# A feed-forward by seven block products instead of eight, and a mixing product cut in two

## The chip, the cores and the metric

One Trainium2 chip, of which the kernel uses one core. The metric is the device time of one execution in microseconds; the time before is the median of three runs. An engine's name stands for its instruction queue: PE (matrix products), DVE and POOL (elementwise), ACT (functions and copies), SP (issues the DMAs).

## What is computed

Two blocks follow each other on 1024 tokens of width 1024, all in float32. Only the parts that the change touches are quoted in full:

```python
def hybrid_layer(x, c, ...):                       # block 1
    ...
    y_att = dsa_attention(...)                     # 8 heads of 64
    y_rwkv = rwkv7_group(...)                      # 8 heads of 64
    mix = jnp.concatenate([y_att, y_rwkv], axis=-1) @ w_out
    x = x + g_m * rms_norm(mix, mix_post_norm)
    hf = rms_norm(x, ffn_pre_norm) * (1 + sc_f) + sh_f
    f = (jax.nn.silu(hf @ w_ffn_gate) * (hf @ w_ffn_up)) @ w_ffn_down   # D_FF = 2816
    return x + g_f * rms_norm(f, ffn_post_norm)
```

Block 2 (`second_block`) normalises that x, multiplies it by `w_in` (a gated convolution, a latent attention and two gates), mixes, adds, and has a feed-forward of its own of the same sizes, with a causal convolution of width 3 in its middle. A gated embedding product ends it.

## The kernel before

**Products.** Every float32 factor is held as two parts, a high one rounded by ACT and a low one, the rest, by a subtraction on POOL or DVE. A product is three MATMULs (high by high, high by low, low by high) summed in PSUM: `mm3`, lines 101 to 103. A MATMUL has 128 rows to contract, 128 columns on the left and 512 on the right.

**Seven for eight.** Where both factors are cut into 2 x 2 blocks, seven products of sums of blocks replace eight. Block 2's feed-forward does so already. `up7` multiplies a weight's block sums by those of the activations, which an `Ops` object holds: per pair of token tiles seven sums of quarters (A11, A12, A22, S1 to S4), each in two parts. `Ops.put` writes rows that come with features on partitions, and `Ops.put_pair` transposes two tiles of tokens, forms the sums and splits them; of its elementwise steps four a pair are POOL's (lines 257, 270, 273). `down7` does the second product: per group of features it loads rows of the weight and of the features, forms the operands with `sub` and `op` (lines 401, 407, 409), multiplies (lines 284 to 286, `mm7`) and adds into accumulators (437, 439). The features lie in DRAM (`f_d`) between the two.

**Mixing.** Attention and RWKV run beside each other; their outputs go to DRAM (`y_att_d`, `y_rwkv_d`). `prologue` brings in the RWKV half (k = 4 to 7 of eight chunks of 128) and its weights while the last attention blocks run, through two raw buffers and four `yl` buffers. Behind attention come the four attention chunks, each multiplied by its softmax reciprocals (`yr`, a broadcast load), and the weights k = 0 to 3. Then per tile of 128 tokens `row_product` sums all eight chunks, 48 MATMULs; `post_add` takes squares (ACT), a root (POOL, lines 110 and 111), scales (DVE, 543) and adds x (POOL, 544); the tile is stored to `x1d`; `renorm` (554, 556) prepares the feed-forward's input, and `put_T` transposes it into `h`, a `Tok`, which holds tokens as they are.

**FFN1.** `ffn1` (lines 514 to 532) goes over 22 chunks of features in groups of two or three: gate and up products by `fm`, SiLU and product, then `down`, which adds to eight accumulators. In the last group `done1` adds x, stores to `x2d`, and `renorm` and `put_T` prepare block 2's input. Block 2's first stage, `local`, reads that and weights of `w_in_2`.

**Order.** No table sets it. The program's order is what the scheduler starts from; it moves an instruction ahead where its operands and buffers allow, and each engine then runs its queue in order. What a tile pool shares memory with, and how many buffers a name has, therefore decides where loads stand on SP. `c.wlayout(a, b)` opens a pool of a raw and b split weight buffers, `c.layout` shares the eight PSUM banks out.

Of the kernel before, what the change touches and what calls it, by code (L numbers as in the profile page):

```python
# [8 lines left out]
FP = mybir.dt.float32  # L9
FR = mybir.dt.float32r  # L10
# [14 lines left out]
class Core:  # L25
# [337 lines left out]

def halves(x):

    x = x.rearrange("p (g e t) -> p g e t", e=2, t=128)
    return x[:, :, 0], x[:, :, 1]


def down7(c, ap, rings, fd, w, nk, done):  # L370
# [9 lines left out]
    def load(k0, n):  # L380
        W, F = wr([128, n, 2, D]), fr([128, n, 2, T])
        for j in range(n):
            for e in range(2):
                k = k0 + 2 * j + e
                nc.sync.dma_start(W[:, j, e], w[k * 128:k * 128 + 128, :])
                nc.sync.dma_start(F[:, j, e], fd[k])
# [37 lines left out]

    ops = ahead(operands(), c.nah)
# [65 lines left out]


def down(c, ap, f, w, k0, kn, acc, first, done):

    nc = c.nc
    wt = [c.split_w(c.load_rows(w, k0 + k)) for k in range(kn)]
    for i in range(NT):
        ps = c.psum([128, D])
        ts = slice(i * 128, i * 128 + 128)
        for hf in range(2):  # L500
            sl = slice(hf * 512, hf * 512 + 512)
            c.mm3(ps[:, sl], [((f[k][:, 0, ts], f[k][:, 1, ts]), (wt[k][:, 0, sl], wt[k][:, 1, sl])) for k in range(kn)])
        if first:
            acc[i] = ap.tile([128, D], FP, name="acc", tag="acc", bufs=NT)
            nc.scalar.activation(acc[i], ps, AF.Copy)
        else:
            nc.vector.tensor_add(acc[i], acc[i], ps)
        done(i)


def ffn1(c, ap, act, wg, wu, wd, groups, done):

    nc = c.nc
    acc, k0 = [None] * NT, 0
    w8 = lambda w, k: c.split_w(c.load_cols(w, k * 128, 128, 8))
    for n, kn in enumerate(groups):
        f, pss = [], []
        if n == 0:
            pss = fms(c, [w8(wg, 0), w8(wu, 0), w8(wg, 1)], 8, act)
        for k in range(k0, k0 + kn):  # L520
            for w in (wg, wu)[max(0, len(pss) - 2 * (k - k0)):]:
                pss.append(fm(c, w8(w, k), 8, act))
            g_ps, u_ps = pss[2 * (k - k0):2 * (k - k0) + 2]
            s = ap.tile([128, T], FP, name="silu", tag="s4", bufs=c.n4)
            nc.scalar.activation(s, g_ps, AF.Silu)
            nc.vector.tensor_mul(s, s, u_ps)  # L526
            ft = ap.tile([128, 2, T], FR, name="fT", tag="s8", bufs=c.n8)
            split(c, s, ft, nc.vector)
            f.append(ft)
        last = n == len(groups) - 1  # L530
        down(c, ap, f, wd, k0, kn, acc, k0 == 0, (lambda i: done(i, acc[i])) if last else (lambda i: None))
        k0 += kn
# [1224 lines left out]
class Via:  # L1757


    def __init__(self, ap):  # L1760
        self.ap, self.more = ap, {}

    def wider(self, ap, **bufs):
        self.other, self.more = ap, bufs

    def tile(self, shape, dt, name, tag=None, bufs=1):
        tag = tag or name
        if tag in self.more:
# [43 lines left out]
def two_layers(ctx, tc, *args):  # L1812
# [28 lines left out]
    with pool("m0") as m0:  # L1841
# [44 lines left out]
        via = Via(at.__enter__())  # L1886
        attend = d.attend(via, lambda pr, t: nc.sync.dma_start(ya[pr], t))
# [11 lines left out]
    h = Tok(hp.__enter__(), "h")  # L1899
    c.layout(qk=(1, 3), tp=(1, 3), o=(1, 2))  # L1900
    c.n4 = 3
    with pool("mo") as ap:
        def prologue():
            for k in range(4, 8):
                wt.append(rows_w(c, ap, p["w_out"], [k], "wo", 4)[0])
                yield
                t = ap.tile([128, T], FP, name="yl", tag="yl", bufs=4)
# [11 lines left out]
        at3.__exit__(None, None, None)
        at.__exit__(None, None, None)  # L1920
        c.layout(ps=(2, 3), tr=(1, 2))
        c.wlayout(2, 1)
        with pool("mo2") as ap2:
            for k in range(4):
                t, r = (ap.tile([128, T], FP, name=n, tag="yl", bufs=4) for n in ("yl", "yr"))
                nc.sync.dma_start(t, ya[k])
                load_rows_over(c, r, d.rd, k)
                nc.vector.tensor_mul(t, t, r)
                h.put(c, k, t)
# [174 lines left out]
```

## Time and profile before

| | |
|---|---|
| Median of three runs | 3802.68 us (3787.42 to 3805.21) |
| The profiled execution's own time | 3790.96 us |
| Its span | 3788.7 us |
| Mean granted clock of PE | 0.88 |
| PE busy | 3314.3 us, 87% |
| DVE, POOL, ACT busy | 51%, 38%, 34% |
| Last attention MATMUL begins | 1165.62 us |
| First and last add of x in mixing begin | 1226.0, 1297.4 us |
| Last MATMUL of FFN1 begins | 2039.46 us |
| Last add of x behind FFN1 begins | 2081.6 us |
| Block 2's feed-forward, first and last MATMUL | 2966.82, 3654.11 us |

The trace has one row for an instruction or a group of them: start and duration in us, the engine, the line of the kernel, what is written and read, and in brackets how long the engine stood idle before it and what ended that. Matmuls overlap: a row of 0.39 us is followed by the next 0.23 us later. The granted clock is a share of 2.4 GHz.

### The profile page before, as it was taken

Reading aid. Unit: us, or ns where it says so; the run is one execution under the profiler, and the core shown is the slowest. Engines: PE = TensorE matmul, PEld = TensorE weight load, DVE = VectorE, ACT = ScalarE, POOL = GpSimd, SP = SyncE. Lnnn points to the kernel's source line nnn. Section 1 sums busy time; section 2 is a strip of 40 time slices with the busy share of each in tenths; the row PEclk is TensorE's granted clock in tenths of the full one; section 3 lists DMA queues with packets and bytes.
Section 4 is the critical chain, followed back from the end, with each engine's and each line's share of the span. In section 5 each row is a group of like instructions: output and inputs, shape, how many; then the busy total and the mean of one; then the engine's idle time right before and its main releaser. Section 6 shows DMA issues by size and latency. Waiting matters only on the chain.

```text
span 3788.7 us, 42125 instructions
## 1 busy us (share of the span) xinstructions
PE 3314.3 (87%) x16048; PEld 2682.2 (71%) x16048; DVE 1946.0 (51%) x3040; ACT 1293.8 (34%) x2177; POOL 1434.0 (38%) x1148
## 2 busy tenths in 40 slices
PE   3787767998996899999997999989978899988878
PEld 2666545676774688888886788778856688866767
DVE  5579977657642312222224200126733688878972
ACT  3355433333333221111113211246623444434332
POOL 3214345434325622222224322131135545438773
PEclk7888765566567899999998999999989899999989
DMA  5552232211214311111113122310143222232334
GB/s 172 153 169 79 82 123 70 73 43 59 54 51 148 127 45 50 50 46 50 51 46 116 53 65 89 110 36 10 54 137 110 85 84 84 84 109 97 111 111 145
DMA packets 252216, 324.65 MB, mean 86 GB/s; under 512 B 16383, under 2 KB 193504, under 8 KB 250992
## 3 DMA queue, kind: packets, MB, share of 16 engines
q1 hardware_dynamic: 250960, 321.75, 26.8%
q8 instruction: 126, 2.06, 0.2%
q14 instruction: 74, 0.61, 0.1%
q0 software_dynamic: 1056, 0.23, 0.0%
HBM read 241.63 MB, written 80.29 MB: 85 GB/s over the span
## 4 chain that ended last, share of the span: by engine, by line
PE 66%; DVE 14%; DMA 6%; POOL 6%; issue 3%; ACT 3%; SPq 0%; POOLq 0%; DVEq 0%; ACTq 0%
PE ps L103 12%; PE ps L101 12%; PE ps L102 12%; PE ps L284 5%; PE ps L286 5%; PE ps L285 5%; DVE junk L840 4%; PE o L591 2%; PE tp L583 2%; DMA adaw<-in_ada_w_dram 1%; PE xy L1284 1%; DVE tmp L1220 1%; POOL acc L544 1%; POOL op L409 1%; PE ra L1195 1%
## 5 line engine op out<-in xcount | busy, mean ns | idle before, releaser
L89 POOL TENSOR_TENSOR whl<-wraw,whl 128x1024 fp32r<-128x1024 f32 (+1 forms) x128 | 285.9, 2238 | 882.5 <-ACT whl L88 879.1
L101 PE MATMUL ps<-h,whl 128*128 128x512 f32 x1216 | 477.3, 395 | 19.4 <-ACT h L210 13.4
L102 PE MATMUL ps<-h,whl 128*128 128x512 f32 x1216 | 477.8, 393 | 3.7 <-POOL h L211 3.7
L103 PE MATMUL ps<-h,whl 128*128 128x512 f32 x1216 | 476.9, 392 | 0.0
L101 PEld LDWEIGHTS ps<-h,whl 128*128 128x128 f32 x1216 | 230.9, 190 | 71.0 <-ACT h L210 15.8
L88 ACT ACTIVATE whl<-wraw 128x1024 fp32r<-128x1024 f32 (+1 forms) x128 | 125.3, 988 | 444.3 <-issue 225.0
L102 PEld LDWEIGHTS ps<-h,whl 128*128 128x128 f32 x1216 | 231.0, 190 | 54.5 <-POOL h L211 6.4
L103 PEld LDWEIGHTS ps<-h,whl 128*128 128x128 f32 x1216 | 230.7, 190 | 47.9
L526 DVE TENSOR_TENSOR silu<-silu,ps 128x1024 f32<-128x1024 f32 x22 | 26.9, 1221 | 434.3 <-PE ps L103 434.3
L286 PE MATMUL ps<-h,op 128*128 128x512 f32 x616 | 240.0, 390 | 2.6 <-POOL op L309 2.6
L284 PE MATMUL ps<-h,op 128*128 128x512 f32 x616 | 237.5, 391 | 5.4 <-ACT op L307 4.4
L285 PE MATMUL ps<-h,op 128*128 128x512 f32 x616 | 240.6, 391 | 0.0
L591 PE MATMUL o<-pT,v 128*128 128x256 f32 (+1 forms) x640 | 155.8, 362 | 14.1 <-ACT pT L586 9.0
L1382 DVE SCALAR_TENSOR_TENSOR cv<-up,v_fw,cv 128x1023 f32<-128x1023 f32 x88 | 150.0, 1705 | 32.0 <-ACT cv L1380 31.0
L586 ACT ACTIVATE pT<-tp 128x512 fp32r<-128x512 f32 (+2 forms) x221 | 94.4, 444 | 185.9 <-PE tp L583 145.5
L284 PE MATMUL ps<-op,op 128*128 128x512 f32 x308 | 122.2, 399 | 36.3 <-ACT op L407 33.2
L101 PE MATMUL ps<-wo,h 128*128 128x512 f32 x320 | 129.4, 413 | 19.2 <-ACT wo L1392 16.2
L102 PE MATMUL ps<-wo,h 128*128 128x512 f32 x320 | 129.5, 410 | 15.5 <-POOL wo L1393 15.5
L591 PEld LDWEIGHTS o<-pT,v 128*128 128x128 f32 x640 | 115.9, 236 | 36.9 <-ACT pT L586 15.0
L840 DVE TENSOR_SCALAR_CACHE_REDUCE junk<-h,tk 128x640 bf16<-128x640 int16 (+7 forms) x128 | 138.0, 1078 | 3.4
L101 PE MATMUL ps<-whl,fT 128*128 128x512 f32 x352 | 137.5, 391 | 0.7 <-DVE silu L526 0.4
L284 PEld LDWEIGHTS ps<-h,op 128*128 128x128 f32 x616 | 116.1, 189 | 30.2 <-ACT op L307 4.8
(596 smaller groups left out, 8279.1 us busy)
## 6 DMA issues: line engine op xcount, KB each, us to landing
wraw<-in_w_ffn_up_dram SPq DMA_DIRECT2D x66, 512.0 KB, 3.9
adaw<-in_ada_w_dram SPq DMA_DIRECT2D x96, 256.0 KB, 3.4
wraw<-in_w_in_dram SPq DMA_DIRECT2D x42, 512.0 KB, 3.9
wraw<-in_w_ffn_gate_dram SPq DMA_DIRECT2D x22, 512.0 KB, 3.9
wraw<-in_w_ffn_down_dram SPq DMA_DIRECT2D x22, 512.0 KB, 3.5
f_d<-cv SPq DMA_DIRECT2D x22, 512.0 KB, 2.6
raw<-in_w_ffn_down_dram SPq DMA_DIRECT2D x22, 512.0 KB, 7.5
raw<-f_d SPq DMA_DIRECT2D x22, 512.0 KB, 5.4
```

What stands on the lines that cost most here:

```text
L88: self.nc.scalar.activation(hl[:, 0], raw, AF.Copy)
L89: self.nc.gpsimd.tensor_sub(hl[:, 1], raw, hl[:, 0].bitcast(FP))
L101: self.nc.tensor.matmul(out, lh, rh, start=first and i == 0, stop=False)
L102: self.nc.tensor.matmul(out, lh, rl, start=False, stop=False)
L103: self.nc.tensor.matmul(out, ll, rh, start=False, stop=last and i == n - 1)
L284: mm(out, lh, rh, start=start and i == 0, stop=False, skip_group_check=True)
L285: mm(out, lh, rl, start=False, stop=False, skip_group_check=True)
L286: mm(out, ll, rh, start=False, stop=stop and i == n - 1, skip_group_check=True)
L586: nc.scalar.activation(pT[:, 0, 0:n, q], x, AF.Copy)
L591: nc.tensor.matmul(o[:, q], v[:, b0 + s].rearrange("p a d -> p (a d)"), pT[:, x, s, q], start=b0 == 0 and n == 0, stop=end and n == 3)
L840: nc.vector.tensor_scalar(junk, x, thr, None, op0=ALU.is_ge, op1=ALU.add, accum_out=out)
L1382: nc.vector.scalar_tensor_tensor(out[:, s:], ps[:, :T - s], w[2 - s][:, j:j + 1], out[:, s:], op0=ALU.mult, op1=ALU.add)
```

## The change

FFN1 is written as block 2's feed-forward is. `ffn1` and `down` go; `h` becomes an `Ops`; `up7` and `features7` write the gated features to a DRAM tensor, and the new class `Down`, which now serves both feed-forwards, runs `down7` with its buffers and calls `done`. `h` as an `Ops` is larger, so weights of the mixing product no longer fit beside it: the RWKV half of that product (k = 4 to 7) is computed on its own in `prologue`, with its split weights in parts of `h` that are not yet written (`h.free`), its sums copied by ACT and stored to `half_d`. The other half is computed per tile behind attention, the stored sum is loaded back and added by DVE. `Via`, which gave attention's tail more buffers, goes. `c.after()` makes the scheduler keep the contraction's loads in the order in which they are written. The core of the diff:

```diff
+    def after(self):
+        return self.tc.issue_after(self.last) if self.last is not None else nullcontext()
...
+class Down:
+    def __enter__(self):
+        self.ap, self.e = self.ap_.__enter__(), self.e_.__enter__()
+        self.c.n4, self.c.nah = 3, 1
...
+    def run(self, fd, w, done):
+        ring = lambda name, dt, a, b: Rings(name, dt, *[(q, n) for q, n in ((self.e, a), (self.ap, b)) if n])
+        raws = ring("raw16", FP, 2, 1)
+        down7(self.c, self.ap, (raws, raws, ring("op8", FR, 4, 4), ring("sm4", FP, 4, 0)), fd, w, fd.shape[0], done)
...
     def load(k0, n):
-        for j in range(n):
...
+        with c.after():
+            for j in range(n):
...
+                    nc.sync.dma_start(W[:, j, e], w[k * 128:k * 128 + 128, :])
+                    c.last = nc.sync.dma_start(F[:, j, e], fd[k]).ins
...
-def down(c, ap, f, w, k0, kn, acc, first, done):
-def ffn1(c, ap, act, wg, wu, wd, groups, done):
-class Via:
...
-    h = Tok(hp.__enter__(), "h")
-    c.layout(qk=(1, 3), tp=(1, 3), o=(1, 2))
+    h = Ops(hp.__enter__(), "h")
+    c.layout(qk=(1, 2), tp=(1, 2), o=(1, 2), ps=(1, 2))
     c.n4 = 3
+    half = tc.dram_tile([T, D], FP, name="half_d")
     with pool("mo") as ap:
         def prologue():
+            wt = []
             for k in range(4, 8):
-                wt.append(rows_w(c, ap, p["w_out"], [k], "wo", 4)[0])
+                wt += rows_w(c, ap, p["w_out"], [k], at={k: h.free(k - 4)})
                 yield
-                t = ap.tile([128, T], FP, name="yl", tag="yl", bufs=4)
+                t = ap.tile([128, T], FP, name="yl", tag="yl", bufs=2)
                 nc.sync.dma_start(t, yd[k - 4])
                 h.put(c, k, t)
                 yield
+            for i in range(NT):
+                t = ap.tile([128, D], FP, name="hm", tag="yl", bufs=2)
+                for hf in range(2):
+                    sl = slice(hf * 512, hf * 512 + 512)
+                    ps = c.psum([128, 512])
+                    c.mm3(ps, [((h.tok(k, 0, i), h.tok(k, 1, i)), (wt[k - 4][:, 0, sl], wt[k - 4][:, 1, sl])) for k in range(4, 8)])
+                    nc.scalar.activation(t[:, sl], ps, AF.Copy)
+                    yield
+                store(half, i, t)
-        c.wlayout(2, 1)
-        beside(ahead, attend, 0.5)
+        c.wlayout(1, 0)
+        beside(ahead1, attend, 0.5)
...
+    with pool("wo1") as wp, pool("mo2") as ap:
+        c.wlayout(2, 0)
+        wt = rows_w(c, wp, p["w_out"], range(4))
+        for k in range(4):
+            t, r = (ap.tile([128, T], FP, name=n, tag="s4", bufs=3) for n in ("yl", "yr"))
...
+        get, get_h = loader(ap, x_in), loader(ap, half, "ht", 2)
+        for i in range(NT):
+            ps = row_product(c, h, wt, i, range(4))
+            y = get_h(i)
+            nc.vector.tensor_add(y, y, ps)
+            xt = get(i)
+            post_add(c, ap, y, xt, G1, xt, y)
+            store(x1d, i, xt)
+            xn = renorm(c, ap, xt, i, None, Gh, Bh)
+            if i % 2:
+                h.put_pair(c, i // 2, xe, xn)
+            xe = xn
+    fd = tc.dram_tile([22, 128, T], FP, name="f_d")
+    c.layout(ps=(1, 8))
+    c.wlayout(4, 7)
+    with pool("f1") as ap:
...
+        for _ in features7(c, ap, up7(c, h, [(load(p["w_ffn_gate"], k), load(p["w_ffn_up"], k)) for k in range(22)]), gated):
+            pass
...
+    with Down(c, pool, "d1") as dn:
...
+        def done1(i, y):
...
+            with c.after():
+                xt = get(i)
+            post_add(c, dn.ap, y, xt, G2, y, y)
+            store(x2d, i, y)
+            h[0].put_T(c, i, renorm(c, dn.ap, y, i, None, Gu), "ps")
+        dn.run(fd, p["w_ffn_down"], done1)
```

How this moves instructions. Ahead of the last attention blocks every engine's order is as before. On **PE**, at the end of attention (`o<-pT` is its last product; `ps<-h` is the half product, both of whose operands lie in `h`; `ps<-wo,h` the other half), the order now reads, with 192 MATMULs of the half in all:

```order
L578 MATMUL o<-pT,v_7528 128x128 x2
L578 MATMUL o<-pT,v_7528 128x256
L105 MATMUL ps<-h 128x512 x2
L106 MATMUL ps<-h 128x512 x2
...
L106 MATMUL ps<-h 128x512
L107 MATMUL ps<-h 128x512
L105 MATMUL ps<-wo,h 128x512 x2
L106 MATMUL ps<-wo,h 128x512
```

Before, `ps<-wo,h` followed attention's last product at once, with all eight chunks of a tile together. Now no MATMUL of the half stands ahead of attention's last.

On **SP**, at the same place, before (`wraw` is a weight's raw buffer, `yl` a chunk of an output, `yr` the reciprocals):

```order
L1890 DMA y_rwkv_d<-yo 128x4x128
L82 DMA wraw<-in_w_out_dram 128x1024
L1908 DMA yl<-y_rwkv_d 128x1024
L82 DMA wraw<-in_w_out_dram 128x1024
L1908 DMA yl<-y_rwkv_d 128x1024 x3
L614 DMA r_att_d<-rsum 16x128
L1887 DMA y_att_d<-yao 128x1024
L82 DMA wraw<-in_w_out_dram 128x1024
...
L1926 DMA yl<-y_att_d 128x1024
L82 DMA wraw<-in_w_out_dram 128x1024 x2
L620 DMA yr<-r_att_d 64x1024 x2
L1893 DMA x1d<-xt 128x1024
```

and now:

```order
L1860 DMA y_rwkv_d<-yo 128x4x128
L82 DMA wraw<-in_w_out_dram 128x1024
L1881 DMA yl<-y_rwkv_d 128x1024 x2
L601 DMA r_att_d<-rsum 16x128
L1857 DMA y_att_d<-yao 128x1024
L82 DMA wraw<-in_w_out_dram 128x1024
L1881 DMA yl<-y_rwkv_d 128x1024
L82 DMA wraw<-in_w_out_dram 128x1024 x2
...
L1863 DMA half_d<-hm 128x1024 x4
L82 DMA wraw<-in_w_out_dram 128x1024 x2
L1863 DMA x1d<-xt 128x1024
L1802 DMA xt<-half_d 128x1024
```

The last two raw weights (k = 2 and 3) moved behind the last store of a half sum, and the loads of k = 4 to 7 stand further apart.

On **SP**, behind the last contraction of FFN1 (`x2d` is the block's output, `in_w_in_dram` here block 2's first weight), before:

```order
L77 DMA wraw<-in_w_in_dram 128x8x128 x2
L1831 DMA xt<-x1d 128x1024
L77 DMA wraw<-in_w_in_dram 128x8x128 x2
L1893 DMA x2d<-acc 128x1024
...
L1831 DMA xt<-x1d 128x1024
L77 DMA wraw<-in_w_in_dram 128x8x128 x3
L1893 DMA x2d<-acc 128x1024
...
L1831 DMA xt<-x1d 128x1024
L1893 DMA x2d<-acc 128x1024
L77 DMA wraw<-in_w_in_dram 128x8x128 x6
```

and now:

```order
L1863 DMA x2d<-acc 128x1024
L1802 DMA xt<-x1d 128x1024
L1863 DMA x2d<-acc 128x1024
...
L1802 DMA xt<-x1d 128x1024
L1863 DMA x2d<-acc 128x1024
L1802 DMA xt<-x1d 128x1024
L1863 DMA x2d<-acc 128x1024
L77 DMA wraw<-in_w_in_dram 128x8x128 x13
```

Block 2's weights, seven of which stood between the stores or ahead of them, are now all behind the last store.

## Rows read from the trace of the kernel before

**Rows 1.** Busy time by engine, the page's part 1: busy us (share) xinstructions.

```profile
PE 3314.3 (87%) x16048; PEld 2682.2 (71%) x16048; DVE 1946.0 (51%) x3040; ACT 1293.8 (34%) x2177; POOL 1434.0 (38%) x1148
```

**Rows 2.** Busy time in five stretches, us (x instructions), then PE's granted clock and DMA.

```profile
1180.00:1200.00 20.00, 11.11 (x29) 8.17 (x30) 3.40 (x2) 5.07 (x5) 16.42 (x7) 0.74 0.96 249
1222.50:1300.00 77.50, 72.23 (x347) 59.95 (x345) 27.93 (x29) 24.14 (x45) 49.33 (x45) 0.99 0.27 95
1400.00:1700.00 300.00, 299.22 (x1318) 246.84 (x1317) 64.06 (x44) 46.90 (x46) 64.54 (x27) 1.00 0.17 50
2975.00:3392.00 417.00, 416.04 (x1836) 344.11 (x1835) 358.93 (x310) 196.43 (x281) 202.93 (x118) 1.00 0.24 77
3413.00:3654.00 241.00, 218.52 (x923) 175.78 (x924) 217.48 (x143) 88.93 (x98) 190.01 (x72) 0.97 0.21 79
```

**Rows 3.** PE in time: start, us, engine, line, out<-in xcount [idle before <-releaser]; the mixing product's start.

```profile
1169.36 1.65 PE L101 MATMUL ps<-wo,h 128*128 128x512 f32 x3 [2.95 <-ACT h L138]
...
1207.08 1.65 PE L101 MATMUL ps<-wo,h 128*128 128x512 f32 x3 [5.55 <-ACT wo L1392]
```

**Rows 4.** DMA issues between 1160 and 1230 us: KB each, median us to landing.

```profile
wraw<-in_w_out_dram SPq DMA_DIRECT2D x8, 512.0 KB, 6.5
...
yr<-r_att_d SPq DMA_DIRECT2D x8, 256.0 KB, 8.9
```

**Rows 5.** SP's queue in time: the first load of the mixing weights.

```profile
1162.48 0.35 SPq L82 DMA_DIRECT2D wraw<-in_w_out_dram  x1
```

**Rows 6.** Groups of POOL between 1160 and 1310 us: busy us, mean ns.

```profile
L1393 POOL TENSOR_TENSOR wo<-wraw,wo 128x1024 fp32r<-128x1024 f32 x8 | 20.7, 2605 | 9.2 <-ACT wo L1392 9.2
...
L544 POOL TENSOR_TENSOR xt<-pa,xt 128x1024 f32<-128x1024 f32 x8 | 19.1, 2384 | 7.2 <-DVE pa L543 5.6 <-issue 1.6
...
L111 POOL TENSOR_TENSOR rs_y<-rs_y,mhalf 128x1 f32<-128x1 f32 x16 | 8.8, 550 | 1.3
```

**Rows 7.** Groups of ACT and of DVE in the same stretch.

```profile
L543 DVE SCALAR_TENSOR_TENSOR pa<-ps,rs_y,G 128x1024 f32<-128x1024 f32 x8 | 10.3, 1283 | 23.6 <-POOL rs_y L111 23.4
...
L115 ACT ACTIVATE sqj<-xt 128x1024 bf16<-128x1024 f32 x8 | 8.4, 1055 | 27.0 <-POOL xt L544 27.0
```

**Rows 8.** POOL's part of `put_pair` in block 2, groups between 2862 and 2957 us.

```profile
L257 POOL TENSOR_TENSOR h<-t,h 128x512 fp32r<-128x512 f32 x6 | 9.5, 1596 | 0.8 <-ACT h L256 0.7
```

**Rows 9.** POOL and DVE in time in that stretch (two answers).

```profile
2918.40 2.40 POOL L544 TENSOR_TENSOR xt<-pa,xt 128x1024 f32<-128x1024 f32 x1
...
2918.47 2.88 DVE L272 TENSOR_TENSOR t<-t,t 128x512 f32<-128x512 f32 x1 [0.26 <-POOL t L270]
2921.27 0.68 DVE L257 TENSOR_TENSOR h<-tr,h 128x512 fp32r<-128x512 f32 x1
```

**Rows 10.** Line 544, which adds x: ns min/median/max, first and last start; block 1's mixing, block 2's.

```profile
L544 POOL TENSOR_TENSOR xt<-pa,xt x8: 2340/2390/2393, 1226.0 to 1297.4; 128x1024 f32<-128x1024 f32 x8
...
L544 POOL TENSOR_TENSOR xt<-pa,xt x8: 2342/2393/2407, 2876.4 to 2954.5; 128x1024 f32<-128x1024 f32 x8
```

**Rows 11.** PE in time: block 1's last MATMUL; block 2's last `up7`, first and last `down7`.

```profile
2039.46 0.39 PE L103 MATMUL ps<-whl,fT 128*128 128x512 f32 x1
...
3392.13 0.39 PE L286 MATMUL ps<-h,op 128*128 128x512 f32 x1
3412.82 1.22 PE L284 MATMUL ps<-op,op 128*128 128x512 f32 x2 [20.30 <-ACT op L407]
...
3654.11 0.39 PE L286 MATMUL ps<-op,op 128*128 128x512 f32 x1
```

**Rows 12.** Waits of PE in block 2's contraction, 3392.6 to 3654 us: total, times, longest.

```profile
PE ps L284 <- ACT op L407: 33.2, 5, 20.3
```

**Rows 13.** Line 544 in the last two tails: FFN1's, block 2's.

```profile
L544 POOL TENSOR_TENSOR acc<-acc,xt x8: 2337/2380/2408, 2017.9 to 2081.6; 128x1024 f32<-128x1024 f32 x8
...
L544 POOL TENSOR_TENSOR acc<-acc,xt x8: 2342/2367/3338, 3653.4 to 3679.8; 128x1024 f32<-128x1024 f32 x8
```

**Rows 14.** Groups of PE between 2057 and 2089.3 us.

```profile
L101 PE MATMUL ps<-h,whl 128*128 128x512 f32 x25 | 10.6, 445 | 0.0
```

More of the change, by code (lines that the diff above doesn't have):

```diff
@@ L1 @@
-from contextlib import ExitStack
+from contextlib import ExitStack, nullcontext
 import concourse.bass as bass
@@ L423, in operands @@
             yield n, op(A22, 1), op(t4, 0)
+    c.last = None
     ops = ahead(operands(), c.nah)
@@ L490, in vectors @@
     return {name: cols[:, s] for name, s in at.items()}
-def down(c, ap, f, w, k0, kn, acc, first, done):
[L495 to L508, printed above, removed]
-def ffn1(c, ap, act, wg, wu, wd, groups, done):
[L513 to L532, printed above, removed]
 def post_add(c, ap, y, x, G, out, t=None):
@@ L1917, in two_layers @@
+        ahead1 = prologue()
+        c.wlayout(1, 0)
+        beside(ahead1, attend, 0.5)
+        for _ in ahead1:
             pass
         c.wlayout()
[L1919 to L1929, printed above, removed]
-            wt = rows_w(c, ap2, p["w_out"], range(4)) + wt
-            ap = ap2
-            G1, Gh, Bh = (row_bcast(c, ap, v, n) for v, n in ((r1, "G1"), (rg, "Gh"), (rb, "Bh")))
-            get = loader(ap, x_in)
-            for i in range(NT):
-                ps = row_product(c, h, wt, i, (4, 5, 6, 7, 0, 1, 2, 3))
-                xt = get(i)
-                post_add(c, ap, ps, xt, G1, xt)
-                store(x1d, i, xt)
-                renorm(c, ap, xt, i, h, Gh, Bh)
@@ L1940, in two_layers @@
-    c.wlayout(3, 4)
-    c.n8, c.n4 = 3, 4
-    with pool("f1") as ap:
-        G2, Gu = row_bcast(c, ap, r2, "G2"), row_bcast(c, ap, p["g_mix_pre_2"], "Gu")
-        get = loader(ap, x1d)
-        def done1(i, y):
-            xt = get(i)
-            post_add(c, ap, y, xt, G2, y, y)
-            store(x2d, i, y)
-            renorm(c, ap, y, i, h, Gu)
-        ffn1(c, ap, h, p["w_ffn_gate"], p["w_ffn_up"], p["w_ffn_down"], (2, 2, 3, 3, 3, 3, 3, 3), done1)
+    at.__exit__(None, None, None)
+    c.layout(ps=(2, 2), tr=(1, 4))
@@ new lines, in two_layers, with gated @@
+    fd = tc.dram_tile([22, 128, T], FP, name="f_d")
+    c.layout(ps=(1, 8))
+    c.wlayout(4, 7)
+    with pool("f1") as ap:
+        c.tp, c.nt2, c.nup = ap, 8, 6
+        load = lambda w, k: lambda: c.load_cols(w, k * 128, 128, 8)
+        def gated(k, x):
+            nc.scalar.activation(x[0], x[0], AF.Silu)
+            yield
+            nc.vector.tensor_mul(x[0], x[0], x[1])
+            nc.sync.dma_start(fd[k], x[0])
+        for _ in features7(c, ap, up7(c, h, [(load(p["w_ffn_gate"], k), load(p["w_ffn_up"], k)) for k in range(22)]), gated):
+            pass
@@ new lines, in two_layers @@
+    c.wlayout()
+    hp.__exit__(None, None, None)
+    c.layout(ps=(2, 4))
+    hp = pool("hp1")
+    with Down(c, pool, "d1") as dn:
+        get = loader(dn.ap, x1d)
+        h = []
+        def done1(i, y):
+            if not h:
+                dn.narrow()
+                h.append(Tok(hp.__enter__(), "h1"))
+                with c.after():
+                    h.extend((row_bcast(c, dn.ap, r2, "G2"), row_bcast(c, dn.ap, p["g_mix_pre_2"], "Gu")))
+            _, G2, Gu = h
+            with c.after():
+                xt = get(i)
+            post_add(c, dn.ap, y, xt, G2, y, y)
+            store(x2d, i, y)
+            h[0].put_T(c, i, renorm(c, dn.ap, y, i, None, Gu), "ps")
+        dn.run(fd, p["w_ffn_down"], done1)
@@ L2050, in done2 @@
             if not h:
-                er.__exit__(None, None, None)
+                dn.narrow()
                 h.append(Tok(hp.__enter__(), "h3"))
-            xt = get(i)
-            post_add(c, ap, y, xt, G4, y, y)
+                with c.after():
+                    h.append(row_bcast(c, dn.ap, p["g_ffn_post_2"], "G4"))
+            G4 = h[1]
+            with c.after():
+                xt = get(i)
+            post_add(c, dn.ap, y, xt, G4, y, y)
             store(x1d, i, y)
             h[0].put_T(c, i, y, "ps")
-        c.nah = 1
-        down7(c, ap, (raws, raws, wrap("op8", FR, 4, 4), wrap("sm4", FP, 4, 0)), fd, p["w_ffn_down_2"], 22, done2)
+        dn.run(fd, p["w_ffn_down_2"], done2)
     h = h[0]
```

56 lines of the change are left out of this document (25 added, 31 removed).

## The prediction

> **What bounds the kernel now.** I read the page's busy times first: PE is busy 87% of the span and no other engine over 51% [rows 1]. That is a mean over stages, so I read a table of stretches next [rows 2]. From 1400 to 1700 us, inside the first feed-forward (FFN1), PE is busy 299.2 of 300 us at the full clock and ran 1318 instructions, 0.227 us each; POOL and DVE are busy about a fifth. Fewer MATMULs there are time won, one for one. The mixing stage before it is different: from 1180 to 1200 PE is busy 11.1 of 20 us at a granted clock of 0.74 (between the 1.2 and 2.4 GHz levels) while POOL is busy 16.4, and PE in time shows why, waiting for POOL or ACT to split a weight [rows 3]. From 1222.5 to 1300 PE has its operands and is busy 72 of 77.5 us. The list of line 544, one add of x per 128 tokens, gives the pace of such tails [rows 10, 13]. Block 2 already does its feed-forward by seven products; its stretches are my templates: 2975 to 3392 (`up7`, PE busy 416 of 417) and 3413 to 3654 (`down7`, PE 218.5 of 241, DVE 217, POOL 190).
>
> All sums are against the profiled execution, 3790.96 us (span 3788.7); the median of the runs shown is 3802.68, 0.3% more, and 0.5% (19 us) is about what a measurement of this kernel can tell from no change.
>
> **1. Fewer MATMULs, by the template.** 22 chunks by up7 are 1848 MATMULs for 2112, by down7 924 for 1056: 396 fewer, at 0.227 us 89.8 us. That is the ceiling. What the stage really takes I copy from block 2. Before, from the end of the last x add of mixing (1297.4 + 2.3 = 1299.7) to FFN1's last MATMUL (2039.7) are 740.0 us [rows 10, 11]. After, from the same add to the end of up7: 2956.9 to 3392.5, 435.6 us [rows 10, 11]; the convolution that keeps DVE at 359 of 417 us there is absent here, but PE did not wait for it, so I take no gain for that. From there to the last down7 MATMUL block 2 needs 3654.3 - 3392.5 = 261.8 us, of which 20.3 is the wait for the first operand [rows 11, 12]. With the loads in order (weight, features, weight, features first) that wait falls: SP's two issues, one 512 KB pair, ACT's first half split, about 7 us, estimated from the 6.5 us that a weight took [rows 4]. So 248.8, together 684.4, and **-55.6 us**. If the first pair were no earlier, this term would be 13 us smaller; if the other PE waits of that stretch, 12.9 us of ACT's 33.2, also went [rows 12], larger by that.
>
> **2. Mixing starts its tiles later.** The half product (k = 4 to 7, 192 MATMULs, 43.5 us at full clock) stands on PE behind the last attention product, not between, so it is not in attention's shade; it fills waits for operands. Its weights come through a single raw buffer. One link is load, ACT, POOL: 4 to 6.5 + 1.06 + 2.6 [rows 4, 6, 7], 8 to 10 us; four links from 1162.5 [rows 5] end at 1195 to 1203. With 36 of the 192 MATMULs done by then, the rest would end at 1230 to 1238; ACT's copies of the half sums stand in one row with the splits of the gated attention output, whose `yr` loads take 8.9 us each [rows 4], so I take 1239. Weights k = 2, 3 are loaded behind the last of the eight stores of half sums: 6.5 + 1.06 + 2 x 2.6 = 12.8 us, of which the second buffer hides none, and 2.7 us of MATMULs. Tile 0's sum is ready at about **1256**. Before it was ready at about 1222.5, where PE's full stretch begins. Bounds: 1244 if half sums end at 1230 and the load takes 4; 1270 below.
>
> **3. The tiles run at another pace.** A tile's product is now 24 MATMULs, 5.4 us, so PE no longer sets the pace, which was (1297.4 - 1226.0) / 7 = 10.2 us [rows 10]. POOL per tile: adds of x and Bh 2 x 2.39, two square roots 2 x 0.55 (their shorter first step left out), and by `put_pair` six us a pair (four steps like L257's 1.6), 3: together 8.9 [rows 6, 8]. That is the lower bound. One tile as a chain (add of the half 1.2, squares 1.25, root 0.55, DVE 1.28, POOL 2.39, and from the squares again) comes to 12.3, with put_pair's 3 that nothing covers 15: the upper. I take 11.2, the spacing of the same steps in block 2's mixing (2876.4 to 2954.5, seven steps [rows 10]), which has the products of 48 MATMULs but one POOL add fewer. From the sum to the end of the x add are 7 us (1.2 + 1.25 + 0.55 + 1.28 + 2.39 and gaps). Tile 7's add ends at 1256 + 78.4 + 7 = 1341.4 for 1299.7: **+41.7 us**.
>
> **4. FFN1's tail.** Before, block 2's first weights were loaded between the tail's stores. The last x2d add began at 2081.6, 7.95 us per tile over the last four [rows 13], yet PE did 73 products (25 per line, 0.227 each, 16.5 us) for block 2 before 2089.3 [rows 14], so block 2 began in effect at 2072.8, 33.1 us after the last MATMUL. After, thirteen of its loads stand on SP behind the last x2d store. Block 2's own tail shows the start: its first x add runs 0.7 us before the last MATMUL's start [rows 11, 13]. Tile 7's add ends at -0.7 + 7 x 7.95 + 2.4 = 57.3, then issue 0.4, load 4 and ACT 1.06: 63 us. **+29.9 us.** Bounds: +47 with a tile slower by a POOL add, +9 if the tiles overlap as far as DVE and POOL allow (two adds like L543's and POOL's 2.39, 5 us a tile).
>
> **5. Block 2's contraction** gets the same order of loads: -13, by term 1; its last weights, for the product after it, are now behind all stores of its tail: +3, estimated from one load's 4 us less one issue. **-10.** Bounds 0 and -20. Everything ahead of attention's last 10 us is the same on each engine: 0. Silu and its product lie beside PE as before; the 22 stores of the features and their loads go to a DMA busy 0.17 to 0.24 [rows 2]: 0, and if that cover were gone a load's 4 us per group of loads, six times, 24.
>
> **Sum:** -55.6 + 41.7 + 29.9 - 10 = +6.0, so 3797 us: what the products save is handed back at the two tails. I call that no change.
>
> **Rivals.**
> *Faster: POOL alone sets the tiles' pace.* Then 8.9 us, and with R = 1244 tile 7's add ends at 1244 + 62.3 + 7 = 1313.3: +13.6 in place of 41.7, 3769 us. With term 4 at its low end, 3749. For it: the order interleaves adds of one tile with roots of the next. Against: ACT and DVE stand between POOL's steps.
> *Slower: the half sums stand in the way.* They and the y tiles share a ring of two buffers, and ACT takes both in one order. If each of the four gated tiles goes alone (yr 8.9, DVE 1.3, ACT 1.06, POOL 2.39: 13.6 us) from 1178, they end at 1232; four tiles of half sums behind them take 4 x 5.4, then the 12.8 + 2.7 of term 2: R = 1270, +14 us, 3811, and with a chain of 12.3 per tile (+7.7) 3819. It decides from R = 1269 on at 11.2 us per tile. For it: the loads of the before trace [rows 4] landed late whenever many were under way. Against: there are three buffers for the gated tiles.
> *Slower: DVE and POOL exclude each other.* In block 2's mixing a DVE subtraction of two SBUF tiles, 128x512, took 2.88 us, beginning with POOL's 2.40 us add and ending 0.55 us after it; the next one, from PSUM, took 0.68 [rows 9]. If every such pair goes one after the other, a tile costs POOL's 8.9 and DVE's 3.6 (two like L543's 1.28 [rows 7], and a pair's three of 0.68): 12.5, and 14 with the gaps that ACT leaves: 3806 to 3817. Before, L543 read PSUM; it now reads the half sum from SBUF. The Trainium skill, "SBUF — State Buffer", section "SBUF: two separate sides", has it as a lock held for a whole instruction, against a VectorE operation with two SBUF inputs. By that rule the pace is 12.5 or more and the sum 3806; by the bare spacing in block 2, 3797; that row agrees with the rule, but block 2's tile has PSUM as an input in this step, so no row shows this stage.
> *The change does not do what it says:* the half product is not in attention's shade; that is in term 2 already.
>
> **How the numbers follow.** Forecast within 10 us of 3797: 0.40. Faster rival 0.28. Ring of half sums 0.16. Exclusion 0.16, a quarter of it within 0.5%. So faster 0.28, same 0.44, slower 0.28. The range takes in the faster rival's ends nearly whole and the slower ones with the 13 us of term 1: 3752 to 3832. The likeliest case alone has 3780 to 3812.
>
> **What would show it.** In the new trace: PE between the last attention product and 1256 with waits for h or hm, 192 MATMULs of the half; the x adds of mixing from 1263 to 1339, 11 us apart; up7 from the last add 435 us later done; the first wait of each contraction about 7 us for 20.3; the last x2d add some 55 us behind the last MATMUL, and block 2's weights loaded after it. Wrong would make it: adds under 9.5 or over 13 us apart, a first add before 1250 or after 1275, or a contraction of block 1 that takes other than 240 to 262 us.

## The result, and the profile after

Over six runs each, the changed kernel takes 3830.57 us (median; 3823.98 to 3837.21) where the kernel before takes 3805.62 (3787.42 to 3810.77): a ratio of 1.0071, interval 1.0048 to 1.0094. It is slower, by 0.7%. I had forecast 3797 us and no change. The profiled execution took 3827.69 us, its span is 3826.0.

The page's busy times, to be set beside [rows 1]:

```profile
PE 3262.9 (85%) x15652; PEld 2630.1 (69%) x15652; DVE 2270.5 (59%) x3333; ACT 1431.6 (37%) x2433; POOL 1660.9 (43%) x1285
```

PE is busy 51 us less, in a span 37 us longer; DVE is busy 324 us more and POOL 227. The 51 us are not all that PE was spared. In FFN1 it is busy 644.8 us for 726.5, 82 less. In the stretches on both sides of FFN1, from the last attention store to the end of mixing's last add of x and from FFN1's last MATMUL to block 2's first gate, it is busy 8 and 9 us longer for nearly the same products, at a mean granted clock of 0.79 for 0.91 and 0.85 for 0.93. Work of the bound did go, and the time went elsewhere. Four stretches of the changed kernel (columns as in [rows 2]): a part of the half product's start, mixing's tiles from the first to the last add of x, up7, and FFN1's contraction.

```profile
1180.00:1200.00 20.00, 11.41 (x24) 6.76 (x24) 0.00 (x1) 4.37 (x5) 9.95 (x5) 0.51 0.48 153
1264.50:1351.20 86.70, 42.48 (x189) 33.97 (x187) 54.30 (x41) 32.01 (x59) 69.55 (x55) 0.78 0.35 121
1400.00:1700.00 300.00, 300.00 (x1325) 248.40 (x1324) 149.33 (x165) 107.02 (x175) 123.90 (x88) 1.00 0.26 82
1798.00:2042.00 244.00, 219.80 (x921) 176.19 (x922) 217.36 (x142) 85.31 (x92) 186.96 (x69) 0.96 0.26 97
```

In up7 PE is busy all of the time at the full clock, as before. In the tiles it is busy 42 of 87 us, where the tiles before kept it busy 72 of 77.5. The adds of x (line 531, before 544) in block 1's mixing and in FFN1's tail, to be set beside [rows 10, 13], and PE in time at the places that the prediction named:

```profile
L531 POOL TENSOR_TENSOR xt<-xt x8: 2344/2364/2388, 1264.5 to 1351.2; 128x1024 f32<-128x1024 f32 x8
...
L531 POOL TENSOR_TENSOR acc<-acc,xt x8: 2341/2344/2412, 2040.0 to 2094.9; 128x1024 f32<-128x1024 f32 x8
```

```profile
1171.00 1.22 PE L105 MATMUL ps<-h 128*128 128x512 f32 x2 [1.04 <-ACT h L237]
...
1195.18 0.79 PE L106 MATMUL ps<-h 128*128 128x512 f32 x1 [1.21 <-POOL h L1380]
...
1243.23 0.73 PE L105 MATMUL ps<-wo,h 128*128 128x512 f32 x2 [4.58 <-ACT wo L1379]
...
1791.23 0.39 PE L290 MATMUL ps<-h,op 128*128 128x512 f32 x1
1797.84 1.22 PE L288 MATMUL ps<-op,op 128*128 128x512 f32 x2 [6.23 <-ACT op L435]
...
2042.50 0.39 PE L290 MATMUL ps<-op,op 128*128 128x512 f32 x1
...
2104.39 0.80 PE L105 MATMUL ps<-h,whl 128*128 128x512 f32 x1 [1.63 <-ACT whl L88]
```

The first row of PE is the half product's first MATMUL, the third the other half's first; then the last of up7, the first and the last of the contraction, and block 2's first. The first wait of the contraction is 6.23 us, where [rows 11] had 20.30 in block 2.

A table by stage, from such rows and from SP's stores; each line but the first is the time from the mark of the line above, in us.

| Mark | before | after | change | forecast |
|---|---|---|---|---|
| Last attention store is issued | 1170.2 | 1171.8 | +1.6 | 0 |
| First x add of mixing | 55.8 | 92.7 | +36.9 | +34.6 |
| Last x add of mixing | 71.4 | 86.7 | +15.3 | +7.0 |
| Last MATMUL of FFN1 ends | 742.3 | 691.5 | -50.8 | -55.6 |
| Block 2's first gate is stored | 182.4 | 213.7 | +31.3 | +29.9 |
| First x add of block 2's mixing | 654.3 | 660.4 | +6.1 | 0 |
| Last features of block 2 are stored | 522.1 | 522.4 | +0.3 | 0 |
| First x add behind block 2's contraction | 254.9 | 247.2 | -7.7 | -13 |
| First x add of the last product | 67.4 | 72.4 | +5.0 | +3 |

### The profile page after: what moved, and what is told of

It reads as the page before. It is cut to its first block, busy times and chain, and to the rows that moved or that the text cites. A ratio compares the mean times of both kernels' runs of the same rounds, so it can differ in the third digit from the quotient of the medians.

```text
span 3826.0 us, 42452 instructions
## 1 busy us (share of the span) xinstructions
PE 3262.9 (85%) x15652; PEld 2630.1 (69%) x15652; DVE 2270.5 (59%) x3333; ACT 1431.6 (37%) x2433; POOL 1660.9 (43%) x1285
## 4 chain that ended last, share of the span: by engine, by line
PE 59%; DVE 15%; POOL 9%; DMA 8%; issue 4%; ACT 4%; SPq 1%; POOLq 0%; DVEq 0%; ACTq 0%
PE ps L288 9%; PE ps L290 9%; PE ps L289 9%; PE ps L107 6%; PE ps L106 6%; PE ps L105 6%; DVE junk L827 3%; PE o L578 2%; POOL op L437 2%; PE tp L570 2%; POOL sm L429 2%; PE xy L1271 1%; DVE sm L429 1%; DMA raw<-f_d 1%; DVE tmp L1207 1%
## 5 line engine op out<-in xcount | busy, mean ns | idle before, releaser
L290 PE MATMUL ps<-h,op 128*128 128x512 f32 x1232 | 480.5, 391 | 5.2 <-POOL op L313 5.2
L288 PE MATMUL ps<-h,op 128*128 128x512 f32 x1232 | 475.0, 391 | 10.9 <-ACT op L311 8.9
L289 PE MATMUL ps<-h,op 128*128 128x512 f32 x1232 | 481.2, 391 | 0.0
L288 PE MATMUL ps<-op,op 128*128 128x512 f32 x616 | 246.6, 403 | 47.8 <-ACT op L435 40.2
L89 POOL TENSOR_TENSOR whl<-wraw,whl 128x1024 fp32r<-128x1024 f32 (+1 forms) x62 | 127.6, 2060 | 348.3 <-ACT whl L88 316.0
L288 PEld LDWEIGHTS ps<-h,op 128*128 128x128 f32 x1232 | 232.5, 189 | 60.6 <-ACT op L311 9.7
L290 PEld LDWEIGHTS ps<-h,op 128*128 128x128 f32 x1232 | 232.3, 189 | 55.0 <-POOL op L313 6.7
L313 POOL TENSOR_TENSOR op<-t,op 128x512 fp32r<-128x512 f32 x88 | 129.8, 1475 | 322.5 <-ACT op L311 322.5
L289 PEld LDWEIGHTS ps<-h,op 128*128 128x128 f32 x1232 | 232.5, 189 | 48.4
L289 PE MATMUL ps<-op,op 128*128 128x512 f32 x616 | 246.8, 402 | 9.0 <-DVE op L437 9.0
L290 PE MATMUL ps<-op,op 128*128 128x512 f32 x616 | 245.4, 400 | 3.8 <-POOL op L437 3.8
L105 PE MATMUL ps<-h,whl 128*128 128x512 f32 x512 | 202.7, 399 | 15.2 <-ACT h L214 13.6
L1692 DVE TENSOR_TENSOR up<-t,ps 128x512 f32<-128x512 f32 x176 | 116.4, 682 | 166.6 <-ACT t L351 121.1
L106 PE MATMUL ps<-h,whl 128*128 128x512 f32 x512 | 204.0, 398 | 3.8 <-POOL h L215 3.8
L107 PE MATMUL ps<-h,whl 128*128 128x512 f32 x512 | 202.8, 396 | 0.2 <-POOL whl L89 0.2
L466 DVE TENSOR_TENSOR acc<-acc,ps 128x1024 f32<-128x1024 f32 x152 | 179.6, 1209 | 15.2 <-PE ps L290 14.3
L288 PEld LDWEIGHTS ps<-op,op 128*128 128x128 f32 x616 | 119.5, 195 | 80.0 <-ACT op L435 46.2
L435 ACT ACTIVATE op<-sm 128x1024 fp32r<-128x1024 f32 (+1 forms) x96 | 91.5, 981 | 185.8 <-POOL sm L429 85.2
```

The lines of the kernel that those rows point to most:

```text
L105: self.nc.tensor.matmul(out, lh, rh, start=first and i == 0, stop=False)
L106: self.nc.tensor.matmul(out, lh, rl, start=False, stop=False)
L107: self.nc.tensor.matmul(out, ll, rh, start=False, stop=last and i == n - 1)
L288: mm(out, lh, rh, start=start and i == 0, stop=False, skip_group_check=True)
L289: mm(out, lh, rl, start=False, stop=False, skip_group_check=True)
L290: mm(out, ll, rh, start=False, stop=stop and i == n - 1, skip_group_check=True)
```

## The experiments

**How far do two executions of the same program differ?** Edit: none. The theory of the prediction was made against one execution, 15 us under the median of the six runs.

> The kernel before, unchanged, profiled a second time, to see how far its stages spread between executions. If stages repeat within a few us, the last x add of mixing begins at 1297 +- 3 us, the last MATMUL of FFN1 742 us after it, the last MATMUL of block 2's contraction at 3654 +- 10, and the span is 3789 +- 10. If the 19 us between the lowest and the highest time of its runs lie in one stage, one of these differences stands out.

Its span is 3801.1 us, 12.4 more. SP's last attention store and the two lists of x adds in that execution:

```profile
1178.82 0.32 SPq L1887 DMA_DIRECT2D y_att_d<-yao  x1
```

```profile
L544 POOL TENSOR_TENSOR xt<-pa,xt x8: 2337/2387/2393, 1234.1 to 1305.5; 128x1024 f32<-128x1024 f32 x8
...
L544 POOL TENSOR_TENSOR acc<-acc,xt x8: 2337/2385/2400, 2026.7 to 2090.4; 128x1024 f32<-128x1024 f32 x8
```

8.6 of the 12.4 us had come by the last attention store (1178.8 for 1170.2), before anything that the change touches. From there, mixing's adds begin at 55.3 and end at 126.7 us where the first execution had 55.8 and 127.2 [rows 10]. So in the kernel before, stages counted from that store repeat to about 1 us, up to FFN1's end. In the changed kernel the first add of x is less steady: 92.7 to 95.8 us from the store in the five profiles that have the half product and its single raw buffer as they are. The stretch from block 2's first gate to its mixing took 657.5 us here for 654.3. In all profiles it lies between 654.0 and 657.5 for the kernel before and its variants, and between 655.4 and 660.4 for the changed kernel and its own, so half of the 6.1 us in the table, or more, may be no effect. Such spread is also why the profiled executions stand 36.7 us apart and the medians 25. Most of the experiments below are a single execution, so they are read by stages and not by their whole time.

**Does the exclusion of DVE and POOL set the tiles' pace?** First the row that shows it in the changed kernel, POOL and DVE in time:

```profile
1307.98 2.34 POOL L543 TENSOR_TENSOR xn<-xn,Bh 128x1024 f32<-128x1024 f32 x1
...
1308.05 3.35 DVE L530 SCALAR_TENSOR_TENSOR xt<-xt,rs_y,G 128x1024 f32<-128x1024 f32 x1 [0.72 <-POOL rs_y L115]
1311.32 1.21 DVE L1917 TENSOR_TENSOR xt<-xt,ps 128x1024 f32<-128x1024 f32 x1
```

The scaling by the root (line 530) begins 0.07 us after POOL's add of Bh and ends 1.08 us after that add's end: 3.35 us for a step that takes 1.28 alone. Behind it on DVE stands the next tile's add of the half sum. All eight in the changed kernel:

```profile
L530 DVE SCALAR_TENSOR_TENSOR xt<-xt,rs_y,G x8: 1279/2813/3402, 1263.1 to 1345.0; 128x1024 f32<-128x1024 f32 x8
```

The experiment puts the sum into PSUM, so that line 530 reads one SBUF tile instead of two:

```diff
-            nc.vector.tensor_add(y, y, ps)
+            nc.vector.tensor_add(ps, ps, y)
             xt = get(i)
-            post_add(c, ap, y, xt, G1, xt, y)
+            post_add(c, ap, ps, xt, G1, xt, y)
```

> The changed kernel, with the half sum added into PSUM instead of SBUF, so that the scaling by the root (line 530) has one SBUF input, not two; the instructions and their sizes stay. If DVE and POOL exclude each other where DVE reads two SBUF tiles: that scaling falls from up to 3.4 us to 1.28, and the x adds of mixing stand 11.2 us apart or less for 12.4, the last of them 8 us earlier or more. If the chain of a tile, or POOL alone, sets the pace: 12.4 us apart as now, the last add within 2 us of 1351.

Time 3820.9 us. The two lines:

```profile
L530 DVE SCALAR_TENSOR_TENSOR xt<-ps,rs_y,G x8: 1274/1284/1285, 1271.6 to 1345.7; 128x1024 f32<-128x1024 f32 x8
...
L531 POOL TENSOR_TENSOR xt<-xt x8: 2342/2379/2803, 1273.1 to 1350.8; 128x1024 f32<-128x1024 f32 x8
```

Line 530 takes 1.28 us every time, and the adds stand (1350.8 - 1273.1) / 7 = 11.1 us apart for 12.4; from the attention store (1178.7) the last is at 172.1 us for 179.4. Work, sizes and order are the same, so these 1.3 us per tile are the exclusion. The Trainium skill states it as a lock for a whole instruction ("SBUF — State Buffer", section "SBUF: two separate sides"); the rows agree, with 3.35 for 1.28.

**More of the same, and the single raw buffer.** Edit, besides the one above:

```diff
-        nc.gpsimd.tensor_add(t, t, b)
+        nc.vector.tensor_add(t, t, b)
...
-        nc.gpsimd.tensor_sub(s3, a11, a21)
+        nc.vector.tensor_sub(s3, a11, a21)
...
-        put(self.S3, s3, nc.gpsimd)
+        put(self.S3, s3, nc.vector)
...
-        c.wlayout(1, 0)
+        c.wlayout(2, 0)
         beside(ahead1, attend, 0.5)
```

> The changed kernel with the half sum added into PSUM as in sum_in_psum, and besides the adds of Bh and the S3 steps of put_pair on DVE instead of POOL (POOL per tile 2.39 + 1.5 + 1.6, DVE's two-input steps 1.28 + 1.37 + 1.7), and two raw buffers instead of one for the half product's weights. If DVE and POOL exclude each other, their sum per tile falls to about 9.8 us and the x adds of mixing stand 9.5 to 10.5 us apart for 11.1; if one tile's chain is next, they stay at 11. If the single raw buffer held the half product back, the first x add comes 84 to 88 us after the last attention store was issued, for 93 to 95; if not, 92 or more.

Time 3806.0 us.

```profile
L531 POOL TENSOR_TENSOR xt<-xt x8: 2343/2402/3445, 1268.1 to 1336.9; 128x1024 f32<-128x1024 f32 x8
```

The adds stand 9.8 us apart. That is what the sum of both engines' steps gives, but POOL's waits in the tiles (total, times, longest) name something else as well:

```profile
POOL xt L531 <- DMA xt<-in_x_dram: 10.1, 5, 2.7
```

Five of the adds waited for the load of x, 10 us in all, where sum_in_psum has 0.3. So the agreement with the sum does not show that the sum is the bound here; a pace set in part by these loads is not ruled out. The first add comes 86.9 us after the attention store (1181.2), 6 to 9 earlier than in the kernels with one raw buffer (92.7 to 95.8 in five profiles), and the half product's last MATMUL begins 60.0 us after the store for 66.4: the single buffer held the half product back by that. The other edits act behind the first add. The last comes at 155.7 for 179.4, 23.7 us earlier. The S3 steps are block 2's too: from its first add of x in mixing to its last store of features it took 519.4 us for 522.4.

**What sets the start of the tiles?** Edit:

```diff
-                    c.mm3(ps, [... for k in range(4, 8)])
+                    c.mm3(ps, [... for k in range(4, 5)])
```

> The changed kernel, whose half product takes one chunk (k = 4) instead of four: 48 MATMULs for 192, with all loads, splits, copies and stores as they are; three quarters of that half are left out of the result. If the half product itself, alone on PE, sets when the tiles start, the first x add comes 23 to 33 us earlier, 60 to 70 us after the last attention store was issued for 93 to 95. If the gated tiles and their broadcast loads hold the start (the last of them is split 57 us after that store), it comes at most 12 us earlier, 82 or later.

Time 3806.9 us.

```profile
L531 POOL TENSOR_TENSOR xt<-xt x8: 2342/2356/2391, 1257.8 to 1343.3; 128x1024 f32<-128x1024 f32 x8
...
1245.76 2.36 POOL L238 TENSOR_TENSOR h<-yl,h 128x1024 fp32r<-128x1024 f32 x1 [2.25 <-ACT h L237]
```

The first x add comes at 1257.8 - 1181.5 = 76.3 us after the attention store, 16 to 19 earlier, between the two expectations. The 144 MATMULs left out are 32.7 us of PE at 0.227; about half of that comes back. PE is idle 8 us in the half product, for ACT's copy of a half sum, then 15.6 us before the other half's first MATMUL, whose weights ACT has not split yet, and in the end it waits for the last gated tile, whose split ends at 1248.1, 66.6 us after the store:

```profile
1192.91 0.79 PE L105 MATMUL ps<-h 128*128 128x512 f32 x1 [8.09 <-ACT hm L1890]
...
1225.90 1.22 PE L105 MATMUL ps<-wo,h 128*128 128x512 f32 x2 [15.59 <-ACT wo L1379]
...
1245.74 1.22 PE L105 MATMUL ps<-wo,h 128*128 128x512 f32 x2 [2.41 <-ACT h L237]
```

So both theories hold in turn: three quarters of the half product cost 16 to 19 us of the 37, and with those gone the start would still be 20 later than before, for the weights and the gated tiles.

**Block 2's weights in FFN1's tail.** Edit, cut to its core (`local` then takes these three for its first product, and the tail's odd tiles are transposed in the PSUM layout of block 2):

```diff
+                c.pre = pool("w2")
+                q = c.pre.__enter__()
+                for col in (512, 1024, 0):
+                    raw = q.tile([128, 8, 128], FP, name="wr2", tag="wr2", bufs=2)
+                    nc.sync.dma_start(raw, p["w_in_2"][:, col:col + 128].rearrange("(k p) n -> p k n", p=128))
+                    hl = q.tile([128, 2, 8, 128], FR, name="wh2", tag="wh2", bufs=3)
...
+            if i == 1:
+                c.layout(ps=(2, 3), tr=(1, 2))
```

> The changed kernel, with block 2's first three weights in buffers of their own, loaded and split during the tail of FFN1, and PSUM shared out for block 2 from the second half of the tail on. If the loads behind the last store are what the tail costs: PE does the 72 MATMULs of the first token half before the last tiles are transposed, and the first store of block 2's gate comes 213 us after FFN1's last MATMUL less 16 to 20, so 194 to 198 us, and the whole is 16 to 20 us shorter. If the chain of the eight tiles is the whole cost: within 3 us of now.

Time 3805.9 us. SP's loads and the tail's adds, then PE before the tail's end:

```profile
2040.27 1.46 SPq L1957 DMA_DIRECT2D wr<-in_w_in_dram  x2
...
2048.56 0.37 SPq L1957 DMA_DIRECT2D wr<-in_w_in_dram  x1
...
L531 POOL TENSOR_TENSOR acc<-acc,xt x8: 2337/2346/2402, 2037.4 to 2099.0; 128x1024 f32<-128x1024 f32 x8
```

```profile
L105 PE MATMUL ps<-h,wh 128*128 128x512 f32 x9 | 4.3, 540 | 0.0
```

The three loads went out at the head of the tail (in the changed kernel they stand behind its last store), and PE had begun on block 2 before the last tile. But the eight adds take 61.6 us for 54.9, since POOL splits the three weights between them. From the tail's first add to block 2's first gate it is 205.9 us for 216.4: 10.5 us won, less than the 16 to 20 expected, and nearly what the tail had lost (204.2 before). The whole came out 22 us shorter, but 4.6 of that lies before the attention store and 5.5 in block 2's contraction, which this edit leaves alone.

**Is the contraction bound by the exclusion too?** Edit:

```diff
-                (G if cnt[0] % 2 else V).tensor_sub(l, x, h.bitcast(FP))
+                (G if cnt[0] % 4 == 1 else V).tensor_sub(l, x, h.bitcast(FP))
```

> The changed kernel, with one low part in four of the contractions' operands subtracted on POOL and three on DVE, for one and one. If POOL and DVE exclude each other, what counts is the sum of POOL's steps at 2.39 us and DVE's two-input steps at 1.37: 41.4 us per full group of four chunks now, 38.3 then, against 38.1 of MATMULs; then each contraction (last product of the features to last MATMUL, 251 us now) takes 235 to 243, the whole is 16 to 30 us shorter, although DVE, at 90% the busiest, gets more work. If DVE's own busy time is the bound, each contraction gets longer, 255 us or more.

Time 3826.9 us. Its contraction in the window table (244 us from just behind the first MATMUL, as for the changed kernel above), its waits of PE, and behind them the same two waits of the changed kernel:

```profile
1804.50:2048.50 244.00, 222.74 (x918) 177.45 (x919) 225.72 (x160) 85.31 (x92) 137.59 (x51) 0.95 0.26 97
```

```profile
PE ps L288 <- ACT op L435: 12.7, 4, 6.4
PE ps L288 <- DVE acc L466: 9.5, 6, 3.7
```

```profile
PE ps L288 <- ACT op L435: 20.2, 5, 7.9
PE ps L288 <- DVE acc L466: 4.1, 4, 1.7
```

POOL's busy time falls from 187 to 138 us, by 18 subtractions. DVE's rises by 8 (225.7 for 217.4), though at the shortest that DVE takes for such a step here, 1.21 us (0.68 for the halved size), they are 20 us: its other steps got shorter, as with the exclusion. But PE waits less for ACT's operands and more for DVE's sums, and from the last store of features to the first add it is 247.4 us for 246.3. Block 2's contraction, which the edit changes too, takes 241.8 us where four of the five profiles that leave it alone have 240.9 to 241.7. Neither expectation: the exclusion is there, and the sum of the two engines' steps isn't what bounds this stretch. What does stays open.

**The order of the loads in a group.** Edit:

```diff
-            for j in range(n):
-                for e in range(2):
+            for e in range(2):
+                for j in range(n):
```

> The changed kernel, where a contraction's group loads the first block of both its chunk pairs before the second, since the first product reads the first block of all of them. If PE's 40 us of idle time in a contraction are waits for the last loads that a product needs (a group's first product then waits for four loads of eight and not for six), a contraction (x add of tile 0 less the last store of features, 246 us in block 1) gets 8 to 15 us shorter, 231 to 238. If POOL and DVE bound it, it stays within 3 us.

Time 3811.4 us. The same waits:

```profile
PE ps L288 <- ACT op L435: 14.2, 4, 6.3
PE ps L288 <- DVE acc L466: 6.5, 2, 3.5
```

242.1 us in block 1, where six profiles with the loads as they were have 243.7 to 247.5; 237.4 in block 2, where they have 240.9 to 247.2: some 4 us each by the middle of these, less than expected. The waits for ACT fall from 20.2 to 14.2 us, those for DVE's sums rise to 6.5.

**One part of the change alone: block 2's loads in order, in the kernel before.** Edit: on the kernel before, the class `Down` and `c.after()`, used for block 2's contraction alone, with the loads of its tail's gain and x behind the contraction's.

> The kernel before, with one part of the change alone: block 2's contraction through the new class, its loads in order and the gain's and x's loads behind them. If that part is worth what the changed kernel's trace shows (first wait 6 us for 20, its tail's last weights later by 5), 8 to 13 us less than the kernel before, a ratio of 0.9965 to 0.998. If the first wait is only moved to later groups: within 3 us.

Over ten runs 3792.83 us for 3802.93, ratio on record 0.9984 (0.9963 to 1.0004; the two medians alone give 0.9973). The interval just takes in 1, so the whole time shows no gain; the stretch does: PE's first wait there,

```profile
3406.63 1.22 PE L288 MATMUL ps<-op,op 128*128 128x512 f32 x2 [7.58 <-ACT op L435]
```

7.58 us for 20.30, and from the last features to the first add 241.5 us for 254.9. With the loads by halves as well:

> The kernel before with block 2's contraction alone changed, as in before_with_ordered_loads and with its loads by halves. It tells how much of all_relieved (ratio 0.9947) is the seven products of FFN1 and how much the contraction's loads. If the loads alone give it, 0.994 to 0.996, and the seven products in FFN1 gain nothing even with their tails relieved. If they give 10 + 4 us, 0.9955 to 0.9975, and FFN1's seven products are worth the rest, 4 to 8 us of their 90.

Over twelve runs 3785.63 us for 3799.66, ratio 0.9966 (0.9952 to 0.998): faster.

**All that helped, on the changed kernel.** Edit: mixing_relieved, weights_in_tail with the low parts of its three weights on DVE, and loads_by_halves.

> The changed kernel with what helped, together: mixing_relieved, weights_in_tail (its low parts on DVE) and loads_by_halves. If the three are independent, 24 + 11 + 8 = 43 us less than the changed kernel: 3784 to 3792 where the kernel before has 3803, a ratio of 0.995 to 0.997. If the tails overlap in what they gain, between 3792 and 3803, and it can't be told from the kernel before.

Over six runs 3782.96 us for 3802.60, ratio 0.9947 (0.9927 to 0.9967): faster than both kernels. Mixing's adds:

```profile
L531 POOL TENSOR_TENSOR xt<-xt x8: 2342/2394/3092, 1266.5 to 1335.5; 128x1024 f32<-128x1024 f32 x8
```

They stand 9.9 us apart. Of its 20 us, 14 can be had without FFN1's seven products (the experiment ahead), another 2 to 3 lie in block 2's mixing and `up7` (519.8 us for 522.4, as in mixing_relieved), and the intervals of the two kernels overlap: that the seven products themselves win anything, even so, is not shown. Nor did all that helped add up: block 2's contraction took 240.9 us here, with its loads by halves, for the 237.4 that they gave alone.

## Why the prediction was wrong

**The step that failed is term 3, the tiles' pace.** It took 11.2 us, the spacing of block 2's tiles, and set the sum of POOL's and DVE's steps aside as a rival. That sum, 12.5, was right: 12.4 was measured, and 11.1 when sum_in_psum took 1.28 out of it. Block 2's spacing was no measure. Here is the stretch that it was read from, in the kernel before, with the columns of [rows 2]:

```profile
2876.40:2954.50 78.10, 73.97 (x355) 61.64 (x353) 40.17 (x36) 34.03 (x62) 48.45 (x47) 1.00 0.27 95
```

PE is busy 74 of the 78 us there, and 48 MATMULs of 0.227 us are 10.9 us of the 11.2. The spacing was PE's: mixing_relieved, with 11 us less of POOL in those tiles, brought it to 10.9 us only. Term 3 had said itself that with 24 MATMULs a tile PE no longer sets the pace. What was left to set it had other operands than in block 2: line 543 reads PSUM there, and POOL has one add fewer. That is 8 us of the miss. The rival "DVE and POOL exclude each other" had named the mechanism; its 3806 to 3817 us fell short too, by the other terms and by the low reference below. None of the signs that were to show the prediction wrong appeared: 12.4 lies between 9.5 and 13, the first add and block 1's contraction inside their bounds. The bounds on the pace were too wide to tell 11.2 from 12.5.

**Term 2** (start at 1256, first add at 1261 to 1263) came out 2.3 us late in this profile, up to 5 in the others. Its reading, that the half product stands alone on PE and that one raw buffer paces it, held: half_cut and mixing_relieved moved the start by 16 to 19 and 6 to 9 us. The rival of the ring of half sums did not decide: the gated tiles were split by 1228.5 us, the half product ended at about 1239, as estimated.

**Term 1**: -50.8 for -55.6. The template held within 1%: 440.3 us from the last x add's start to the end of up7, for 438 in block 2, and 251.2 us of contraction for 248.8. The first wait was 6.23, forecast 7. From mixing's last add of x to FFN1's last MATMUL, before and now:

```profile
1299.70:2039.70 740.00, 726.50 (x3192) 598.80 (x3192) 154.38 (x112) 134.40 (x141) 176.36 (x86) 0.99 0.19 57
```

```profile
1353.50:2042.70 689.20, 644.76 (x2780) 526.47 (x2780) 435.61 (x380) 240.27 (x346) 369.63 (x198) 0.97 0.26 87
```

PE is busy 82 us less and idle 44 us for 13.5; some 30 us of that idle time are the contraction's waits for its operands. So what 89.8 us of MATMULs bring is some 51. The runs show the loads as a part of those waits and rule out POOL's share as their bound.

**Term 4**: +31.3 for +29.9. The adds stood 7.84 us apart (forecast 7.95), block 2's first MATMUL came 61.7 us after the last of FFN1 (forecast 63). weights_in_tail won back 10.5 us.

**Term 5**: the contraction -7.7 in the changed kernel's profile, -13.2 to -14.0 in the four other profiles that left it alone; forecast -13. The last weights cost 5, forecast 3.

**The reference.** Against the medians the change costs 25 us. The terms above miss by 8 (pace), 2, 5, 1 and 2 (term 5 by the four other profiles), together 18 on top of the +6.0 of the forecast. The rest of the 36.7 between the two profiles is spread: of attention and of the way to block 2's mixing, as before_again shows it, and the 5 to 6 us by which the changed kernel's profile had a longer contraction in block 2 than those four. Of the 34 us between the forecast time and the measured median, 15 are the profile of before, which stands 0.4% under its runs' median. That offset should have been written into the range, not only into a sentence; the range takes in the measured time only just, and by luck: it was not made for this offset.

## What to carry to other kernels

Before taking a pace from another stage, look which engine set it there: block 2's tiles were paced by PE, the new ones had half its work. Before costing an elementwise step by a row of another stage, compare where its operands lie: in these tiles two SBUF inputs on DVE beside a busy POOL cost close to the sum of both (3.35 us for 1.28), one from PSUM did not (1.28). A product cut in two gains only if the first half finds idle time early enough; here it ran behind attention, and leaving out three quarters of it brought the tiles 16 to 19 us forward. When matrix work shrinks at both ends of a stage, count the tails first: 90 us of MATMULs went, 83 came back at a start and two tails, and more than the rest in the contraction's waits.

## What the runs showed of the hardware that was not expected

Letting DVE write a sum into PSUM costs next to nothing (1.23 us for the add, 1.21 before) and took 9 us out of eight tiles. In the contraction, taking 49 us of subtractions from POOL raised DVE's busy time by 8 us, where its shortest rows would make them 20: rows of DVE beside a busy POOL hold waiting in their durations, so its 217 us of 244 was not a measure of its work.
